# Tuned two-layer decoder kernel: ScalarE reads shared banks first, values between the halves of layer B's keys, both key parts in one product in layer A's first tile

## The chip, the cores and the metric

The kernel runs on one core of one Trainium2 chip. The metric is the device time of one launch in microseconds (us), the median of several runs. A core has five engines with queues of their own: TensorE (PE) multiplies matrices and transposes, and writes into the eight banks of PSUM; ScalarE (ACT) and VectorE (DVE) read those banks and work on tiles in SBUF; GpSimd (POOL) works on SBUF alone; SyncE (SP) issues most of the transfers. Each engine takes its instructions in order and stands still at an instruction whose semaphores are not yet set.

## What is computed

A trunk of two layers on 512 tokens of width 1024. Layer A is latent attention with 8 heads (causal, query blocks of 128), layer B sliding-window attention with 16 query heads on 4 key heads. Each is followed by a layer norm, an MLP with squared ReLU and another layer norm. Cut to what the change touches:

```python
# layer A, one block i of 128 queries of one head
s = einsum('bqhc,bkc->bhqk', ql, c_kv) + einsum('bqhr,bkr->bhqk', qr, k_r)
p = softmax(where(kpos <= qpos, s * scale, -inf))
# layer B
k, v = split(x @ w_kv)          # 4 heads of 64, shared
q = x @ w_q                     # 16 heads of 64
s = einsum(q, k_band) * scale   # block n sees key blocks n-1 and n
p = softmax over (s + bias) and one learned sink per head
```

## The kernel before

Everything is float32 to the eye, but each operand of a product is held as two rounded parts, a high one and a low one (`split`: ScalarE copies the high part, VectorE or GpSimd subtracts it from the source), and a product is made of three: high by high, high by low, low by high (`three`, `group`). PE keeps its program order as it is written (`pe`). On the other engines the builder's scheduler orders the instructions by priority and by what they wait for, and it lets a second engine read a bank only behind the first one's read of it. There are six banks of the tag `mm` and two of the tag `tr` for transposes.

Weights come as a stream of pieces of 128x1024 (`queue`, `weights`): a transfer, a copy to `wh`, a subtraction to `wl`.

Layer A's attention (`scores`, `turn`, `mix` under `run_steps`) goes by head h and query block i. `scores(h, i)` multiplies the queries by n = 128(i+1) keys with five products: `kh` and `kl` with `qh`, `kh` with `ql`, and the rotary parts `khh` and `kll` with `qr`. At i = 0 all five are 128 columns wide. VectorE then adds the mask and takes the maximum in one reduction, and ScalarE takes the exponential.

Layer B begins (`begin`) with two chunks of keys and two of queries, each in two halves of 256 tokens. The first half is multiplied while the last two tiles of tokens are still being turned (`turn_tokens`), in the order keys 0, keys 1, turn 2, queries 0, turn 3, queries 1; then all four second halves, then the values of token tile 0. Values 1 to 3 are fill work in the attention.

Layer B's attention goes by head. I call two heads that share a query chunk a pair, m = 0 to 7 (heads 2m and 2m+1); chunk m of the queries is fill work of two parts of 12 products, 512 columns wide. So PE repeats, for each head, what I call a half: 7 transposes of an earlier head's probabilities (`turn`, L1284 and L1286), 8 products with the values (`mix`), 8 products for the scores of a later head (`scores`), and one part of a query chunk. Behind part 1 stands `query_parts` (L1227, L1228): for each of the two heads ScalarE copies 64 partitions of the bank into `q`, and VectorE subtracts that copy into the other 64. VectorE's work for one head is four reductions with the bias (L1256, one of 128 and three of 256 columns), the bound `nb` (L1260), the low parts `ptl` of the turned probabilities (two pieces, 512 and 384 columns) and the sum `o`. ScalarE's is four exponentials `p` (L1264), the high parts `pth`, and `low`. The last pair, m = 7, has parts of the output projection (`proj`, products of `wh`/`wl` with `oh`/`ol`) as fill in place of queries.

Of the kernel before, what the change touches and what calls it, by code (L numbers as in the profile page):

```python
# [48 lines left out]
def build(tc, nc, io, out):  # L49
    with ExitStack() as top:  # L50
# [231 lines left out]
        first_sq = len(stream)  # L282
        for m in range(8):
            queue("w_sq", io["w_sq"][m], nc.gpsimd if m > 1 else nc.vector, m < 2)
            if m == 1:
                for half_ in range(2):
                    queue("w_v", io["w_v"][half_])
# [70 lines left out]
        for i in range(2):  # L358
            at_hand[i] = raw_tile()
            fetched.add(i)  # L360
            for c in (slice(0, 320), slice(320, 640)) if i == 0 else (slice(0, 640),):
                pe(nc.scalar.dma_start(at_hand[i][:, c], io["w_kv"][i][:, c]))
# [211 lines left out]
        def begin(src, chunks):  # L574


            state["hold"] = len(stream)
            ws = [weights(name) for name, _ in chunks]
            late = []
            for half_ in range(2):  # L580
                cols = slice(half_ * 256, half_ * 256 + 256)
                for i, (_, evac) in enumerate(chunks):
                    b = bank(256)
                    feat_major(src, ws[i], b, cols)
                    late.append((evac, cols, b))
                    if half_ == 0 and i in (1, 2):
                        with tc.high_priority():
                            src.turn(i + 1)
                    if half_ or i > 2:

                        with behind(src.last if not half_ else None):
                            for evac, *at in late:
                                evac(*at)
                        late = []
# [27 lines left out]
        class XFactors(Factors):  # L622
# [14 lines left out]
            def turn(self, t):  # L637

                half_, tk = t // 2, slice(t % 2 * P, (t % 2 + 1) * P)
                if t == NT - 1:  # L640
                    self.b = self.scratch()
                    with tc.issue_after(self.low[1].ins):
                        nc.vector.tensor_sub(self.b, f32(self.xf[0][:, 1]), f32(self.xf[0][:, 0]))
                if t % 2 == 0:
                    self.xf[half_] = self.mp.tile([P, 2, 4, 256], F32R, tag="fac", bufs=3, name=nm("xf"))
                pts = []
                for n in range(2):
                    pt = tbank().rearrange("p (a b) -> p a b", a=4)
                    pts.append(pt)
                    for a in range(4):  # L650
                        k = n * 4 + a
                        pe(nc.tensor.transpose(pt[:, a, :], xs[t][:, k * P : (k + 1) * P], ident))  # L652
                    if half_ == 0:
                        split(self.part(n + 1, 0)[:, :, tk], self.part(n + 1, 1)[:, :, tk], pt)
                    nc.scalar.activation(f32(self.xf[half_][:, n, :, tk]), pt, AF.Copy)
                if half_ == 1:
                    if t % 2 == 0:
                        self.a = self.scratch()
                    nc.vector.tensor_sub(self.a[:, :, tk], pts[0], f32(self.xf[1][:, 1, :, tk]))
                    if t == NT - 1:  # L660
                        nc.vector.tensor_add(self.b[:, :, tk], self.b[:, :, tk], self.a[:, :, tk])
                    self.low = split(self.part(5, 0)[:, :, tk], self.part(5, 1)[:, :, tk], self.a[:, :, tk], keep=True)
                if t == NT - 1:
                    for i in (1, 0):
                        tk = slice(i * P, (i + 1) * P)
                        if i == 0:
                            with tc.issue_after(self.low[1].ins):
                                nc.vector.tensor_add(self.b[:, :, tk], self.b[:, :, tk], self.a[:, :, tk])
                        state["s4"] = split(self.part(3, 0)[:, :, tk], self.part(3, 1)[:, :, tk], self.b[:, :, tk], keep=True)
                    state["hold"] = len(stream)  # L670
# [11 lines left out]
        def mlp(src, gb, dst, mp):  # L682
# [177 lines left out]
            if dst is not None:  # L860
                state["hold"] = first_sq
# [5 lines left out]
        with tc.tile_pool(name="mla", bufs=1) as mp:  # L867
# [9 lines left out]
            khh = mp.tile([P, S], F32R, name="khh")  # L877
            kll = mp.tile([P, S], F32R, name="kll")
# [47 lines left out]
            kr2 = [mp.tile([P, NT, P], F32, tag=("kh", "kl")[a], bufs=2, name=nm("kr2")) for a in range(2)]  # L926

            def rot_key(t, b):
                kr = sp.tile([P, 2, 64], F32, tag="kr", bufs=2, name=nm("kr"))
                rope(kr[:, 0, :], b[:, 256:320], t, 1, kr[:, 1, :])  # L930
                dup = kr[:, 0:1, :].broadcast_to([P, 2, 64])
                hh = kr2[0][:, t, :].rearrange("p (a b) -> p a b", a=2)
                ll = kr2[1][:, t, :].rearrange("p (a b) -> p a b", a=2)
                nc.vector.tensor_copy(hh.bitcast(F32R), dup)
                nc.vector.tensor_sub(ll, dup, hh)
# [41 lines left out]
            for t in range(NT):  # L977
# [12 lines left out]
                if t == 2:  # L990
                    with tc.high_priority():
                        for part, dst in ((0, khh), (1, kll)):
                            pt = tbank()
                            for tt in range(NT):
                                pe(nc.tensor.transpose(pt[:, tt * P : (tt + 1) * P], kr2[part][:, tt, :], ident))
# [22 lines left out]
            def head_keys(h):  # L1018
                heads[h]["w"] = wh, wl = weights("w_h")
                kh = mp.tile([P, S], F32R, tag="kh", bufs=2, name=nm("kh"))  # L1020
                kl = mp.tile([P, S], F32R, tag="kl", bufs=2, name=nm("kl"))
# [4 lines left out]
                split(kh, kl, b)  # L1026
                heads[h]["k"] = kh, kl
# [12 lines left out]
            def pair_rotary(hp):  # L1040

                pt = bank()
                for t in range(NT):
                    pe(nc.tensor.transpose(pt[:, t * P : (t + 1) * P], qrot[t // 2][:, t % 2, hp * P : (hp + 1) * P], ident))  # L1044
                for j, (own, other) in enumerate(((lo, hi), (hi, lo))):
                    qr = mp.tile([P, S], F32R, tag="qr", bufs=3, name=nm("qr"))
                    nc.scalar.activation(qr[own, :], pt[own, :], AF.Copy)
                    nc.vector.tensor_sub(qr[other, :], pt[own, :], f32(qr[own, :]))
                    heads[2 * hp + j]["qr"] = qr
# [25 lines left out]
            def scores(h, i):  # L1075
                a = heads[h]
                kh, kl = a["k"]
# [4 lines left out]
                group(  # L1082
                    b[:, :n],
                    three(qh[:, tq], ql[:, tq], kh[:, :n], kl[:, :n])
                    + [(a["qr"][:, tq], khh[:, :n]), (a["qr"][:, tq], kll[:, :n])],
                )
                if i == 0:
# [5 lines left out]
                    out=b[:, :n], in0=b[:, :n], in1=cmask[:, 512 - n :], op0=ALU.add, op1=ALU.max,  # L1093
# [3 lines left out]
                p = scratch()  # L1097
# [76 lines left out]
        with tc.tile_pool(name="swa", bufs=1) as mp:  # L1174
# [3 lines left out]
            def keys(m, cols, b):  # L1178
                for a, (own, other) in enumerate(((lo, hi), (hi, lo))):
                    j = 2 * m + a  # L1180
                    for to in (own, other):
                        nc.scalar.activation(khh[j][to, cols], b[own, :], AF.Copy)
                        nc.vector.tensor_sub(kll[j][to, cols], b[own, :], f32(khh[j][own, cols]))
# [6 lines left out]
            def values(t):  # L1190
                if t == 0:
                    wv.extend(weights("w_v") for _ in range(2))
                tk = slice(t * P, (t + 1) * P)
                b = bank(256)
                for k in range(KD):
                    wh, wl = wv[k // 4]
                    c = slice(k % 4 * 256, (k % 4 + 1) * 256)
                    group(b, three(x2.h(k, tk), x2.l(k, tk), wh[:, c], wl[:, c]), k == 0, k == 7)
                split(vv[:, t, :, 0:64], vv[:, t, :, 64:P], b.rearrange("p (j d) -> p j d", j=4))
# [13 lines left out]
            def queries(m, part):  # L1213
# [4 lines left out]
                if part == 1:  # L1218
                    load_bias(m)
                    query_parts(m, slice(0, S), b)  # L1220

            def query_parts(m, cols, b):
                if qs[2 * m] is None:
                    qs[2 * m : 2 * m + 2] = [mp.tile([P, S], F32R, tag="q", bufs=4, name=nm("q")) for _ in range(2)]
                for a, (own, other) in enumerate(((lo, hi), (hi, lo))):
                    q = qs[2 * m + a]
                    nc.scalar.activation(q[own, cols], b[own, :], AF.Copy)  # L1227
                    nc.vector.tensor_sub(q[other, cols], b[own, :], f32(q[own, cols]))  # L1228
# [91 lines left out]
            for m in range(2, 8):  # L1320
                for part in range(2):
                    fill.append((2.6, 2 * m - AHEAD_B - 3 + part, -9, lambda m=m, part=part: queries(m, part)))
                if m == 2:
                    for t in range(1, NT):
                        fill.append((2.6, 0, -9, lambda t=t: values(t)))
            for t, kp, u in ((0, 0, 11), (0, 1, 12), (1, 0, 13), (1, 1, 13), (2, 0, 14), (2, 1, 14), (0, 2, 15), (1, 2, 15), (2, 2, 16)):
                fill.append((1.3 if t < 2 else 0, u, u, lambda t=t, kp=kp: proj.part(t, kp)))
            for m in range(2):
                load_bias(m)
            begin(  # L1330
                x2,
                [("w_k", lambda cols, b, m=m: keys(m, cols, b)) for m in range(2)]
                + [("w_sq", lambda cols, b, m=m: query_parts(m, cols, b)) for m in range(2)],
            )
            values(0)
# [118 lines left out]
```

## Time and profile before

| | |
|---|---|
| median of 3 runs | 1004.05 us (1003.70 to 1004.14) |
| the profiled execution | 1003.37 us, its span 1001.6 us |
| TensorE's granted clock | 0.998 |
| PE busy | 989.3 us, 99% of the span |
| DVE, ACT, POOL busy | 771.0, 555.3, 216.0 us |

Busy PE is no measure of PE at its best, since products are pipelined and their ends are modelled. What a product costs is read from the time between two starts. Where that time is longer than between other products of the same widths, PE stood still, and the row says in brackets what ended its wait.

### The profile page before, as it was taken

To read this page: it belongs to the slowest core of one execution; us is meant where nothing else is said; L and a number is where in the kernel's file an instruction comes from. 1 tells how busy PE (TensorE), PEld (TensorE's weight loads), DVE (VectorE), ACT (ScalarE), POOL (GpSimd) and SP (SyncE) were. 2 spreads that over 40 slices of the span, in tenths; PEclk is the share of its full clock that TensorE was granted. 3 is DMA by queue.
4 is the path that set the end of the run, shared out by engine and by line. 5 is a ranking of instruction groups with operands and counts; after the bars stand their busy time and mean duration, and the time that the engine had idled before them with its cause. 6 is when DMAs were issued, how large, how long until landed. Compare 5 with 4: busy or idle time off the path is not lost.

```text
span 1001.6 us, 15947 instructions
## 1 busy us (share of the span) xinstructions
PE 989.3 (99%) x6172; PEld 893.1 (89%) x6172; DVE 771.0 (77%) x1237; ACT 555.3 (55%) x851; POOL 216.0 (22%) x203
## 2 busy tenths in 40 slices
PE   9999999999999999999999999999999999999997
PEld 8888888999999999998899988889998999999986
DVE  5588866989779769886586678698885986898756
ACT  5456643458537637646146788446763764664620
POOL 1231101112212211210003665212122032122000
PEclk9999999999999999999999999999999999999999
DMA  6431126389978977964232212258798798798432
GB/s 247 144 99 43 64 106 210 87 178 243 168 168 227 187 175 203 225 120 135 76 105 96 85 64 75 73 180 199 188 195 185 167 213 171 169 263 146 105 105 84
DMA packets 60392, 149.56 MB, mean 149 GB/s; under 512 B 5228, under 2 KB 10013, under 8 KB 60317
## 3 DMA queue, kind: packets, MB, share of 16 engines
q0 software_dynamic: 24320, 58.73, 32.9%
q1 hardware_dynamic: 35564, 89.16, 26.3%
q8 instruction: 49, 0.80, 0.3%
q10 hardware_dynamic: 432, 0.66, 0.2%
q14 instruction: 27, 0.21, 0.1%
HBM read 146.41 MB, written 4.22 MB: 150 GB/s over the span
## 4 chain that ended last, share of the span: by engine, by line
PE 96%; ACT 2%; DVE 1%; issue 1%; DMA 0%; DVEq 0%; ACTq 0%
PE mm L104 88%; PE tr L104 5%; PE tr L1114 1%; PE tr L652 1%; ACT wh L77 1%; PE tr L1284 0%; ACT p L1264 0%; DMA xraw<-in_xT 0%; PE tr L432 0%; PE tr L1286 0%; ACT q L1227 0%; DVE wl L80 0%; PE mm L1044 0%; PE tr L908 0%; DVE ql L80 0%
## 5 line engine op out<-in xcount | busy, mean ns | idle before, releaser
L104 PE MATMUL mm<-wh,fac 128*128 128x512 f32 (+1 forms) x944 | 292.4, 386 | 0.0
L77 ACT ACTIVATE wh<-wq 128x1024 fp32r<-128x1024 f32 x164 | 173.6, 1060 | 185.5 <-PE mm L104 129.3
L80 DVE TENSOR_TENSOR wl<-wq,wh 128x1024 fp32r<-128x1024 f32 x164 | 199.4, 1220 | 69.4 <-ACT wh L77 68.3
L104 PE MATMUL mm<-xth,wh 128*128 128x256 f32 (+1 forms) x944 | 246.8, 289 | 0.7 <-ACT p L1264 0.7
L104 PE MATMUL mm<-xth,wl 128*128 128x256 f32 (+1 forms) x816 | 236.1, 289 | 0.0
L104 PEld LDWEIGHTS mm<-wh,fac 128*128 128x128 f32 x944 | 176.2, 188 | 35.4 <-DVE fac L80 0.6
L104 PE MATMUL mm<-xtl,wh 128*128 128x256 f32 (+1 forms) x688 | 199.9, 291 | 0.0
L104 PE MATMUL mm<-wl,fac 128*128 128x512 f32 (+1 forms) x472 | 182.3, 386 | 0.0
L104 PEld LDWEIGHTS mm<-xth,wh 128*128 128x128 f32 x944 | 171.7, 192 | 4.1 <-ACT p L1264 1.5
L104 PEld LDWEIGHTS mm<-xth,wl 128*128 128x128 f32 x816 | 156.3, 192 | 2.0
L77 ACT ACTIVATE wh<-raw 128x1024 fp32r<-128x1024 f32 (+4 forms) x85 | 84.7, 998 | 99.0 <-PE mm L104 66.8
L104 PEld LDWEIGHTS mm<-xtl,wh 128*128 128x128 f32 x688 | 131.8, 192 | 2.4
L199 POOL DMA_DIRECT2D wq<-in_up x64 | 77.5, 1228 | 258.8 <-DVE wl L80 192.5
L80 DVE TENSOR_TENSOR wl<-raw,wh 128x1024 fp32r<-128x1024 f32 (+3 forms) x65 | 76.8, 1188 | 38.1 <-ACT wh L77 37.9
L104 PEld LDWEIGHTS mm<-wl,fac 128*128 128x128 f32 x472 | 88.8, 188 | 16.7
L199 POOL DMA_DIRECT2D wq<-in_down x48 | 42.0, 875 | 187.1 <-DVE wl L80 181.2
L80 POOL TENSOR_TENSOR wl<-raw,wh 128x1024 fp32r<-128x1024 f32 (+2 forms) x20 | 41.3, 2071 | 86.7 <-ACT wh L77 84.3
L104 PE MATMUL mm<-wh,oh 128*128 128x512 f32 x128 | 51.1, 399 | 0.9 <-ACT p L1264 0.9
L104 PE MATMUL mm<-wh,ol 128*128 128x512 f32 x128 | 50.1, 392 | 0.0
L104 PE MATMUL mm<-wl,oh 128*128 128x512 f32 x128 | 49.9, 390 | 0.0
L393 POOL TENSOR_TENSOR rs<-mv,half 128x1 f32<-128x1 f32 x16 | 9.9, 620 | 168.2 <-DVE mv L414 168.1
L558 DVE TENSOR_TENSOR x<-mm,x 128x512 f32<-128x512 f32 (+1 forms) x49 | 32.8, 673 | 15.0 <-PE mm L104 15.0
(217 smaller groups left out, 1844.1 us busy)
## 6 DMA issues: line engine op xcount, KB each, us to landing
wq<-in_up POOLq DMA_DIRECT2D x64, 512.0 KB, 8.6
wq<-in_down POOLq DMA_DIRECT2D x48, 512.0 KB, 6.8
wq<-in_up SPq DMA_DIRECT2D x32, 512.0 KB, 7.2
raw<-in_down SPq DMA_DIRECT2D x28, 512.0 KB, 6.6
wq<-in_down SPq DMA_DIRECT2D x24, 512.0 KB, 5.7
raw<-in_up SPq DMA_DIRECT2D x16, 512.0 KB, 4.3
raw<-in_w_o SPq DMA_DIRECT2D x8, 512.0 KB, 3.9
raw<-in_w_sq SPq DMA_DIRECT2D x8, 512.0 KB, 3.3
```

The lines of the kernel that those rows point to most:

```text
L77: high = nc.scalar.activation(dst_h, src, AF.Copy)
L80: low = (engine or nc.vector).tensor_sub(dst_l, src, f32(dst_h))
L104: pe(nc.tensor.matmul(dst, st, mv, start=first and i == 0, stop=last and i == len(pairs) - 1, **kw))
L199: nc.gpsimd.dma_start(half(a, jp), chunk(*more, jp), accum_op=ALU.add)
L393: nc.gpsimd.tensor_tensor(r, v, half, ALU.pow)
L558: nc.vector.tensor_add(xs[t][:, c], b, xs[t][:, c])
L652: pe(nc.tensor.transpose(pt[:, a, :], xs[t][:, k * P : (k + 1) * P], ident))
L1114: pe(nc.tensor.transpose(pt[:, kb * P : (kb + 1) * P], p[:, kb * P : (kb + 1) * P], ident))
```

## The change

Five edits. In layer A the two parts of a head's keys lie in one tile `kk`, and those of the rotary key in one tile `krr`. At i = 0 one product of `qh` with both parts of `kk` writes 256 columns of the bank, one of `qr` with `krr` adds to them, and one of `ql` with the high part adds to the first 128. VectorE adds the second 128 columns and the mask into `p`, and the reduction takes `p` for its mask. At i > 0 the five products stay.

Layer B starts with keys 0 and 1 of the first half; the turns of tiles 2 and 3 have the values of token tiles 0 and 1 between and behind them, half of the inner dimension each; then come the second halves of the keys, then query chunks 0 and 1 whole, 512 columns wide. The weights of the values come ahead of those of the queries in the stream. Values 2 and 3 stay fill work.

Where ScalarE and VectorE both read a bank in several pieces (`XFactors.turn`, `keys`, `query_parts`, `pair_rotary`), ScalarE's pieces all come first, then VectorE's. In layer B's attention `query_parts` has high priority. At the kernel's start the second piece of `w_kv` is fetched on SP's queue, behind the third transfer of `xT`, where it went out on ScalarE's queue before.

```diff
-                kh, kl = a["k"]
+                kk = a["k"]
+                p = scratch()
+                mask = cmask[:, 512 - n :]
+                if i == 0:
+                    two = b[:, 0:256].rearrange("p (a b) -> p a b", a=2)
+                    group(
+                        two, [(qh[:, tq], kk[:, :, :n]), (a["qr"][:, tq], krr[:, :, :n])], True, False,
+                        skip_group_check=True,
+                    )
+                    group(b[:, :n], [(ql[:, tq], kk[:, 0, :n])], False, True, skip_group_check=True)
+                    nc.vector.tensor_add(p[:, :n], b[:, n : 2 * n], mask)
+                    mask = p[:, :n]
...
+            late = products(0)
+            for i, f in enumerate(between):
+                with tc.high_priority():
+                    src.turn(NT - 2 + i)
+                late += f()
+
+            with behind(src.last):
+                for evac, *at in late:
+                    evac(*at)
+            for evac, *at in products(1):
+                evac(*at)
...
                 if part == 1:
                     load_bias(m)
-                    query_parts(m, slice(0, S), b)
+                    with tc.high_priority():
+                        query_parts(m, slice(0, S), b)
...
-                for a, (own, other) in enumerate(((lo, hi), (hi, lo))):
-                    q = qs[2 * m + a]
+                sides = [(qs[2 * m + a], own, other) for a, (own, other) in enumerate(((lo, hi), (hi, lo)))]
+                for q, own, _ in sides:
                     nc.scalar.activation(q[own, cols], b[own, :], AF.Copy)
+                for q, own, other in sides:
                     nc.vector.tensor_sub(q[other, cols], b[own, :], f32(q[own, cols]))
...
-                    for t in range(1, NT):
-                        fill.append((2.6, 0, -9, lambda t=t: values(t)))
+                    for t in range(2, NT):
+                        fill.append((2.6, 0, -9, lambda t=t: more_values(t)))
...
-            begin(
-                x2,
-                [("w_k", lambda cols, b, m=m: keys(m, cols, b)) for m in range(2)]
-                + [("w_sq", lambda cols, b, m=m: query_parts(m, cols, b)) for m in range(2)],
-            )
-            values(0)
+            begin(
+                x2, ["w_k"] * 2, [lambda cols, b, m=m: keys(m, cols, b) for m in range(2)],
+                [lambda half_=half_: first_values(half_) for half_ in range(2)],
+            )
+            for m in range(2):
+                for part in range(2):
+                    queries(m, part)
```

PE, layer A, the first block of a head (`mm` is the bank of the scores), before:

```order
L104 MATMUL mm_743<-cq_170,wl_608 128x512
L104 MATMUL mm_755<-kh_612,qh_695 128x128
L104 MATMUL mm_755<-kl_613,qh_695 128x128
L104 MATMUL mm_755<-kh_612,ql_696 128x128
L104 MATMUL mm_755<-khh,qr_718 128x128
L104 MATMUL mm_755<-kll,qr_718 128x128
L104 MATMUL mm_779<-ckv_h,wh_624 128x512
```

The same place after:

```order
L104 MATMUL mm_739<-cq_169,wl_606 128x512
L104 MATMUL mm_751<-kk_610,qh_692 128x256
L104 MATMUL mm_751<-krr,qr_715 128x256
L104 MATMUL mm_751<-kk_610,ql_693 128x128
L104 MATMUL mm_773<-ckv_h,wh_621 128x512
```

Five products of 128 columns have become two of 256 and one of 128; what stands around them is the same.

DVE, layer B's attention, the half behind the end of query chunk 6 (`q` are its two heads' queries, `ISA` the reductions with the bias, `ptl` the low parts of the turned probabilities), before:

```order
L1260 TENSOR_SCALAR nb_6276<-mm_6279,sink_155 128x4
L1228 TENSOR_TENSOR q_6318<-mm_6235,q_6318 64x512
L80 TENSOR_TENSOR ptl_6325<-tr_6326,pth_6324 128x512
L1256 ISA mm_6356<-mm_6356,bias_6164 128x128
...
L1256 ISA mm_6356<-mm_6356,bias_6164 128x256
...
L1256 ISA mm_6361,mm_6356<-mm_6361,bias_6164 128x256
...
L1256 ISA mm_6361,mm_6356<-mm_6361,bias_6164 128x256
...
L80 TENSOR_TENSOR ptl_6325<-tr_6333,pth_6324 128x384
L1260 TENSOR_SCALAR nb_6353<-mm_6356,sink_155 128x4
L1314 TENSOR_TENSOR o_6263<-mm_6339,low_6348 64x512
L1228 TENSOR_TENSOR q_6319<-mm_6235,q_6319 64x512
```

The same place after:

```order
L1297 ISA mm_6280<-mm_6280,bias_6088 128x128
...
L1297 ISA mm_6280<-mm_6280,bias_6088 128x256
...
L1297 ISA mm_6285,mm_6280<-mm_6285,bias_6088 128x256
...
L1269 TENSOR_TENSOR q_6242<-mm_6159,q_6242 64x512
L1269 TENSOR_TENSOR q_6243<-mm_6159,q_6243 64x512
L1297 ISA mm_6285,mm_6280<-mm_6285,bias_6088 128x256
...
L80 TENSOR_TENSOR ptl_6249<-tr_6250,pth_6248 128x512
L80 TENSOR_TENSOR ptl_6249<-tr_6257,pth_6248 128x384
L1355 TENSOR_TENSOR o_6187<-mm_6263,low_6272 64x512
L1301 TENSOR_SCALAR nb_6277<-mm_6280,sink_155 128x4
```

The first subtraction for the queries stood ahead of the reductions and the second behind `o`; now both stand behind the third reduction, and ahead of both pieces of `ptl`.

DVE, the same half of the last pair, behind query chunk 7 (`wl` is a piece of the projection's weights), before:

```order
L80 TENSOR_TENSOR wl_6535<-raw_6533,wh_6534 128x1024
L1228 TENSOR_TENSOR q_6470<-mm_6387,q_6470 64x512
L80 TENSOR_TENSOR ptl_6477<-tr_6478,pth_6476 128x512
L1256 ISA mm_6508<-mm_6508,bias_6316 128x128
...
L1256 ISA mm_6508<-mm_6508,bias_6316 128x256
...
L1256 ISA mm_6513,mm_6508<-mm_6513,bias_6316 128x256
...
L80 TENSOR_TENSOR ptl_6477<-tr_6485,pth_6476 128x384
L1314 TENSOR_TENSOR o_6415<-mm_6491,low_6500 64x512
```

The same place after:

```order
L1297 ISA mm_6432<-mm_6432,bias_6240 128x128
...
L80 TENSOR_TENSOR wl_6459<-raw_6457,wh_6458 128x1024
L1297 ISA mm_6432<-mm_6432,bias_6240 128x256
...
L1269 TENSOR_TENSOR q_6394<-mm_6311,q_6394 64x512
L1269 TENSOR_TENSOR q_6395<-mm_6311,q_6395 64x512
L80 TENSOR_TENSOR ptl_6401<-tr_6402,pth_6400 128x512
L1297 ISA mm_6437,mm_6432<-mm_6437,bias_6240 128x256
...
L80 TENSOR_TENSOR ptl_6401<-tr_6409,pth_6400 128x384
```

`wl` and the first subtraction stood ahead of the reductions; now `wl` stands behind the first reduction, and both subtractions behind the second.

## Rows read from the trace of the kernel before

**Rows 1.** The page: busy time of the engines, and the chain that ended last.
```profile
PE 989.3 (99%) x6172; PEld 893.1 (89%) x6172; DVE 771.0 (77%) x1237; ACT 555.3 (55%) x851; POOL 216.0 (22%) x203
...
PE 96%; ACT 2%; DVE 1%; issue 1%; DMA 0%; DVEq 0%; ACTq 0%
```

**Rows 2.** PE's waits, whole span: total us, times, longest us.
```profile
PE mm L104 <- ACT p L1264: 1.6, 6, 0.7
```

**Rows 3.** Timeline of PE, layer A's first block: start, duration, instruction, [idle before, releaser].
```profile
80.31 0.30 PE L104 MATMUL mm<-kh,qh 128*128 128x128 f32 x1
80.45 0.28 PE L104 MATMUL mm<-kl,qh 128*128 128x128 f32 x1
80.56 0.28 PE L104 MATMUL mm<-kh,ql 128*128 128x128 f32 x1
80.67 0.27 PE L104 MATMUL mm<-khh,qr 128*128 128x128 f32 x1
80.78 0.27 PE L104 MATMUL mm<-kll,qr 128*128 128x128 f32 x1
```

**Rows 4.** Timeline of PE, second halves at the start of layer B.
```profile
524.28 0.28 PE L104 MATMUL mm<-xth,wh 128*128 128x256 f32 x1
524.40 0.28 PE L104 MATMUL mm<-xtl,wh 128*128 128x256 f32 x1
```

**Rows 5.** Timeline of PE, one half of layer B's attention, from its first transpose.
```profile
605.28 0.27 PE L1284 MATMUL tr<-ident,p 128*128 128x128 f32 x1
...
607.92 0.40 PE L104 MATMUL mm<-xth,wh 128*128 128x512 f32 x1
608.15 0.40 PE L104 MATMUL mm<-xtl,wh 128*128 128x512 f32 x1
...
610.67 0.27 PE L1284 MATMUL tr<-ident,p 128*128 128x128 f32 x1
```

**Rows 6.** Timeline of PE, layer B's attention, three places where it stands still.
```profile
601.97 0.28 PE L104 MATMUL mm<-skl,q 128*128 128x256 f32 x1
602.43 0.50 PE L104 MATMUL mm<-xth,wh 128*128 128x512 f32 x1 [0.18 <-ACT p L1264]
...
615.46 0.27 PE L1286 MATMUL tr<-ident,p 128*128 128x128 f32 x1
616.33 0.30 PE L1284 MATMUL tr<-ident,p 128*128 128x128 f32 x1 [0.60 <-DVE ptl L80]
...
622.52 0.28 PE L104 MATMUL mm<-skl,q 128*128 128x256 f32 x1
623.50 0.50 PE L104 MATMUL mm<-wh,oh 128*128 128x512 f32 x1 [0.71 <-ACT p L1264]
```

**Rows 7.** Timeline of DVE, the same stretch.
```profile
601.13 0.69 DVE L1228 TENSOR_TENSOR q<-mm,q 64x512 fp32r<-64x512 f32 x1 [1.32 <-ACT q L1227]
601.85 0.69 DVE L80 TENSOR_TENSOR ptl<-tr,pth 128x512 fp32r<-128x512 f32 x1
602.46 0.29 DVE L1256 CUSTOM_DVE_ANT_0 mm<-mm,bias 128x128 f32<-128x128 f32 x1
...
602.79 0.43 DVE L1256 CUSTOM_DVE_ANT_0 mm<-mm,bias 128x256 f32<-128x256 f32 x1
...
603.37 0.43 DVE L1256 CUSTOM_DVE_ANT_0 mm<-mm,bias 128x256 f32<-128x256 f32 x1
...
607.64 0.30 DVE L1256 CUSTOM_DVE_ANT_0 mm<-mm,bias 128x128 f32<-128x128 f32 x1
...
608.94 0.42 DVE L1256 CUSTOM_DVE_ANT_0 mm<-mm,bias 128x256 f32<-128x256 f32 x1
...
609.28 0.56 DVE L80 TENSOR_TENSOR ptl<-tr,pth 128x384 fp32r<-128x384 f32 x1
...
611.73 1.22 DVE L80 TENSOR_TENSOR wl<-raw,wh 128x1024 fp32r<-128x1024 f32 x1 [0.70 <-ACT wh L77]
```

**Rows 8.** Timeline of ACT, the same stretch.
```profile
600.51 0.59 ACT L1227 ACTIVATE q<-mm 64x512 fp32r<-64x512 f32 x1
```

**Rows 9.** Timeline of PE, the kernel's start.
```profile
10.87 0.31 PE L104 MATMUL mm<-wh,xth 128*128 128x320 f32 x1
11.20 0.41 PE L104 MATMUL mm<-wl,xth 128*128 128x320 f32 x1
```

More of the change, by code (lines that the diff above doesn't have):

```diff
@@ L281, in build @@
             queue("w_k", io["w_k"][m])
-        first_sq = len(stream)
+        first_v = len(stream)
+        for half_ in range(2):
+            queue("w_v", io["w_v"][half_], after=True)
         for m in range(8):
[L284 to L287, printed above, removed]
+            queue("w_sq", io["w_sq"][m], nc.gpsimd if m > 1 else nc.vector)
         for c in range(8):
@@ L356, in build @@
         state["hold"] = len(stream)
[L358 to L362, printed above, removed]
+        at_hand[0] = raw_tile()
+        fetched.add(0)
+        for c in (slice(0, 320), slice(320, 640)):
+            pe(nc.scalar.dma_start(at_hand[0][:, c], io["w_kv"][0][:, c]))
         prep(0, 2, lambda j: load_x(j, 1))
@@ L572, in feat_major, with begin, products @@
                 group(dst, three(wh[:, kc], wl[:, kc], src.h(k, cols), src.l(k, cols)), k == 0, k == KD - 1)
-        def begin(src, chunks):
+        def begin(src, names, evacs, between):
             state["hold"] = len(stream)
[L578 to L582, printed above, removed]
+            ws = [weights(name) for name in names]
+            def products(half_):
+                late = []
+                for w, evac in zip(ws, evacs):
+                    cols = slice(half_ * 256, half_ * 256 + 256)
                     b = bank(256)
-                    feat_major(src, ws[i], b, cols)
+                    feat_major(src, w, b, cols)
                     late.append((evac, cols, b))
[L586 to L594, printed above, removed]
+                return late
+            late = products(0)
[8 more added lines that the diff above has]
+                evac(*at)
         class Factors:
@@ L860, in mlp @@
             if dst is not None:
[L861 removed]
+                state["hold"] = first_v
             TokMajor(Hidden(), add_last, "down").finish(gb, dst, dst and (0, 0, 0, 1))
@@ L923, in rope @@
                 nc.vector.tensor_add(dst, dst, other)
-            kr2 = [mp.tile([P, NT, P], F32, tag=("kh", "kl")[a], bufs=2, name=nm("kr2")) for a in range(2)]
+            kr2 = mp.tile([P, 2, NT, P], F32, tag="kk", bufs=2, name=nm("kr2"))
             def rot_key(t, b):
@@ L994, in build @@
                             for tt in range(NT):
-                                pe(nc.tensor.transpose(pt[:, tt * P : (tt + 1) * P], kr2[part][:, tt, :], ident))
+                                pe(nc.tensor.transpose(pt[:, tt * P : (tt + 1) * P], kr2[:, part, tt, :], ident))
                             nc.scalar.activation(dst, pt, AF.Copy)
@@ L1019, in head_keys @@
                 heads[h]["w"] = wh, wl = weights("w_h")
-                kh = mp.tile([P, S], F32R, tag="kh", bufs=2, name=nm("kh"))
-                kl = mp.tile([P, S], F32R, tag="kl", bufs=2, name=nm("kl"))
+                heads[h]["k"] = kk = mp.tile([P, 2, S], F32R, tag="kk", bufs=2, name=nm("kk"))
                 b = bank()
@@ L1044, in pair_rotary @@
                     pe(nc.tensor.transpose(pt[:, t * P : (t + 1) * P], qrot[t // 2][:, t % 2, hp * P : (hp + 1) * P], ident))
+                qr = [mp.tile([P, S], F32R, tag="qr", bufs=3, name=nm("qr")) for _ in range(2)]
+                for j, own in enumerate((lo, hi)):
+                    nc.scalar.activation(qr[j][own, :], pt[own, :], AF.Copy)
                 for j, (own, other) in enumerate(((lo, hi), (hi, lo))):
[L1046 to L1049, printed above, removed]
+                    nc.vector.tensor_sub(qr[j][other, :], pt[own, :], f32(qr[j][own, :]))
+                    heads[2 * hp + j]["qr"] = qr[j]
             values_in()
```

68 lines of the change are left out of this document (40 added, 28 removed).

## The prediction

> **What bounds the kernel now.** I read the page's chain first: PE carries 96% of it and is busy 99% of the span [rows 1]. So a part of the change counts if it takes time from PE's own row of products, or moves one of the few places where PE stands still. Then I read PE's waits: the largest entry is ScalarE's exponential of layer B's attention, 1.6 us in six waits [rows 2]. Last comes the timeline around these waits, for the work that is queued ahead of what PE wants.
>
> A wait is measured start to start. Between two products of 256 columns 0.12 us pass [rows 4], and a 512-column product also starts about 0.12 behind one of 256. At 601.97 it took 0.46 [rows 6]: 0.34 of waiting, and some 0.1 more because the product after a pause is longer, 0.50 for 0.40 [rows 5, 6]. So 0.45, and five of the six waits look alike, one for each of the pairs 3 to 7. The sixth is 0.98 at 622.52, about 0.95 above the normal step; ahead of it stand 0.87 at 615.46, where transposes wait for `ptl`, 0.76 above their 0.11 [rows 6]. Layer B's attention thus loses 5 x 0.45 + 0.76 + 0.95, about 4.0 us. There is as much to lose there as to gain.
>
> **Layer A's first block.** Five products of 128 columns follow each other at 0.11 [rows 3]; two of 256 and one of 128 take 2 x 0.12 + 0.11 = 0.35 for 0.55. That is 0.20 for each of 8 heads: -1.6 us, on PE itself. No row shows a right-hand operand in two pieces; at i = 0 each piece is one run of 128 columns, so I take 0.12, with nothing gained as the other end (0.22, two products of 128). VectorE gets 8 additions of 128 columns, about 0.3 each by the 128-column reduction [rows 7]. What waits for them is the exponential, whose block is turned only three blocks later, so I cost them at nothing; uncovered they would be 8 x 0.3 = 2.4.
>
> The Trainium skill gives two paces ("TensorE: Matmul & The Clock Gate", Back-to-back issue gap): an isolated product takes N/2.4 + 2.5 ns, and a sustained stream about 81 ns for 128 columns and 131 for 512. By the first, joining products would gain almost nothing here; by the second the queries below alone would gain some 3 us. This trace agrees with neither: 110 ns for 128 columns, 120 for 256, 229 for 512. The rows decide.
>
> **Layer B's start.** The two query chunks were 96 products of 256 columns, 11.5 us at 0.12. Now they are 48 of 512: 12 took 2.75 us, from 607.92 to 610.67 [rows 5], so 48 take 11.0: -0.5. The values of tile 1 only move ahead. The values do between the turns what the first query halves did, and their weights have the old place in the stream. The second key half needs what it needed; the first query chunk then needs weights whose buffer comes free when keys 0 end, 2.9 us (24 x 0.12) ahead; a copy and a subtraction (1.22, [rows 7]) fit in with some 0.4 to spare. If that cover is gone it costs the shortfall, hardly over 0.5. Scores 0 want queries 0, which end one whole chunk (5.5 us) earlier. I cost this at nothing.
>
> **Layer B's attention.** In the half behind a query chunk's end I count from its first transpose. The scores' first reduction starts at 2.36 (605.28 to 607.64), and the next half is due at 5.39 (605.28 to 610.67) [rows 5, 7]. Before, the first subtraction for the queries ran ahead of the reductions, where VectorE had been idle 1.32 us, and the second much later [rows 7]; ScalarE's second copy waited for the first subtraction, so the query bank stayed taken and the next chunk waited for a scores bank, that is for the exponential. After, both copies stand together, and in the order of pairs 5 and 6 both subtractions stand behind the third reduction and ahead of `ptl`. The next half's transposes wait for `ptl`, since they write the bank that it reads. By the steps of rows 7: 2.36, then 0.33 and 0.58 to the third reduction, 0.34 to the subtractions, 2 x 0.72, 0.34 for the fourth reduction, 0.61 for `ptl`: 6.0. PE waits 0.6 where it waited 0.45: +0.17 for each of pairs 5 and 6. In pair 3 the exponential keeps its place, with one copy more ahead of it (up to 0.59, [rows 8]): +0.5. In pair 4 the copies fall behind the exponential, and by the same count 0.2 remains: -0.25.
>
> Pair 7 is the worst. `wl` (1.22) stood in the idle time ahead of the reductions [rows 7]; now it stands behind the first, with both subtractions behind the second: 2.36 + 0.33 + 1.2 + 0.34 + 1.44 + 0.61 = 6.3, while PE, with only six products of projection between (6 x 0.23), is there at about 4.0. That is 2.3, then 0.35 for the second piece of `ptl`, and about 0.7 of the later wait for the exponential: 3.35 against 0.45 + 0.76 + 0.95 = 2.15, so +1.2. The attention together: 0.5 - 0.25 + 0.35 + 1.2 = **+1.8**. Its bounds: -2.25 if the five waits go and nothing takes their place, +3 if the subtractions also delay the exponentials.
>
> **The start.** The second piece of `w_kv` no longer competes with the third transfer of `xT`, so that copy can start sooner. Of this PE sees the step at 10.87, 0.33 where 0.15 is normal [rows 9]: -0.2. If the piece itself comes late by one issue, it is +0.4.
>
> **Reader order elsewhere.** PE has no wait over 0.1 at the two turns to the MLPs or at the keys; the subtractions that come one copy (about 0.6) later have over 1 us until their products. Nothing.
>
> **Sum.** -1.6 - 0.5 + 1.8 - 0.2 = -0.5. The profiled execution took 1003.37, so 1002.9; the median stands 0.7 above it: **1003.5**.
>
> **Rivals.** (a) *The attention loses nothing*: the scheduler's new order leaves no wait longer than the old. Then the total is -2.3 and better: 1001.7 at an attention of 0, 999.5 with the five waits gone. For it: the query bank is really freed sooner. Against it: VectorE's order in pairs 5 to 7. It is faster by the bound if the attention costs under +0.3. Chance 0.27.
>
> (b) *VectorE becomes the bound of the pairs*: in each of the five pairs the two subtractions (1.44) come wholly on PE's path, since `nb`, the exponential and GpSimd's scaling also wait behind them. That is 5 x 1.44 for 5 x 0.45, +5.0, and +1.2 at the end: in all 6.2 - 2.3, so 1008. It is slower than before once the pairs and the end lose 2.3, slower by the bound from 4.3. Against it: VectorE has time to spare in each pair, 1.32 us ahead of one subtraction alone [rows 7]. Chance 0.07.
>
> (c) *Joining does not pay*: a product costs by its columns, or one in two pieces costs two. Then -1.6 is lost: 1005.1. The page's first pace is of this kind. Against it: 0.11 and 0.12 in rows 3 and 4. Chance 0.05.
>
> **How the numbers follow.** My forecast, within 1002.1 to 1005, has 0.61. Under 0.2% (2.0 us) nothing can be told from no change. Faster by more: 0.27, from (a); slower by more: 0.07, from (b); the same: 0.61 + 0.05. The range for 8 in 10 reaches into (a) and ends below (b): 1000.9 to 1005.3.
>
> **What would show it.** In the profile after: two 256-column steps of 0.12 and one of 0.11 in layer A's first block; 24 products of 512 columns in a row for each of query chunks 0 and 1 without a pause at either front; in the attention waits of transposes for `ptl` in pairs 5 and 6 (about 0.6 each) and one over 2 us in pair 7, where the exponential's waits were. If those transposes do not wait, my reading of VectorE's queue is wrong, and (a) holds. If PE waits for the exponential in every pair, (b) does.

## The result, and the profile after

The kernel after takes **1006.73 us** (1005.99 to 1007.43, 10 runs) where the kernel before took 1003.98 beside it (10 runs): ratio **1.0026**, interval 1.0016 to 1.0036. It is slower by 2.75 us. The forecast of 1003.5 was wrong, and the time lies above the range.

The page of the kernel after, and PE's waits (total us, times, longest us):

```profile
PE 986.9 (98%) x6108; PEld 889.4 (89%) x6108; DVE 774.8 (77%) x1241; ACT 555.4 (55%) x847; POOL 217.1 (22%) x203
...
PE 93%; DVE 3%; ACT 1%; DMA 1%; issue 1%; POOL 0%; DVEq 0%; POOLq 0%; ACTq 0%
```

```profile
PE tr L1325 <- DVE ptl L80: 5.4, 5, 3.3
...
PE mm L104 <- ACT p L1305: 0.9, 1, 0.9
```

PE does 64 products fewer and is busy 2.4 us less than in [rows 1], yet the span grew from 1001.6 to 1004.4 us. In the chain PE's share fell from 96 to 93%, and VectorE's rose from 1 to 3%. The six waits for the exponential of [rows 2] have become one, and in their place stand five waits of the transposes for `ptl`, 5.4 us together (before, one of 0.6). So I looked first at what came before these waits, then at the waits.

**What was gained.** Layer A's first block after the change, on PE, for the head of [rows 3]:

```profile
79.96 0.36 PE L104 MATMUL mm<-kk,qh 128*128 128x256 f32 x1
80.16 0.28 PE L104 MATMUL mm<-krr,qr 128*128 128x256 f32 x1
80.28 0.22 PE L104 MATMUL mm<-kk,ql 128*128 128x128 f32 x1
```

From `krr` to the next start 0.12 pass, as between products of 256 columns in one piece. The block's three products take 0.38 (79.96 to 80.34), where the five took 0.58 (80.31 to 80.89): 0.20 for each head, as forecast. The product `mm<-wh,oh` that starts at 176.37 before starts at 174.53 after: 1.84 us earlier. Layer B's first two query chunks are now 48 products of 512 columns in a row, at 0.23 to 0.24 each (528.64 to 539.55), without a pause at either front:

```profile
528.64 0.40 PE L104 MATMUL mm<-xth,wh 128*128 128x512 f32 x1
528.88 0.40 PE L104 MATMUL mm<-xtl,wh 128*128 128x512 f32 x1
```

The last scores product ahead of the first wait starts at 565.96 (below) where it started at 568.33 before:

```profile
568.33 0.28 PE L104 MATMUL mm<-skl,q 128*128 128x256 f32 x1
```

By then the change is 2.37 us ahead, of which 0.5 came since 499 us. These two terms are as forecast.

**What was lost.** PE in layer B's attention, the same places as in [rows 6], one fence for pairs 3 to 7 (the idle time and its releaser in brackets):

```profile
565.96 0.28 PE L104 MATMUL mm<-skl,q 128*128 128x256 f32 x1
567.17 0.50 PE L104 MATMUL mm<-xth,wh 128*128 128x512 f32 x1 [0.93 <-ACT p L1305]
...
581.18 0.30 PE L1325 MATMUL tr<-ident,p 128*128 128x128 f32 x1 [0.23 <-DVE ptl L80]
...
592.99 0.30 PE L1325 MATMUL tr<-ident,p 128*128 128x128 f32 x1 [0.82 <-DVE ptl L80]
...
604.78 0.30 PE L1325 MATMUL tr<-ident,p 128*128 128x128 f32 x1 [0.82 <-DVE ptl L80]
...
614.02 0.39 PE L104 MATMUL mm<-wh,ol 128*128 128x512 f32 x1
617.75 0.30 PE L1325 MATMUL tr<-ident,p 128*128 128x128 f32 x1 [3.34 <-DVE ptl L80]
...
618.11 0.27 PE L1327 MATMUL tr<-ident,p 128*128 128x128 f32 x1
618.56 0.30 PE L1325 MATMUL tr<-ident,p 128*128 128x128 f32 x1 [0.18 <-DVE ptl L80]
```

Start to start, over the normal step, these are 1.1 (1.2 with the longer product behind it), 0.39, 0.97, 0.97, and in pair 7 3.50 and 0.35. That is 7.3 us. The last wait of [rows 6] is gone.

Then TensorE's clock falls. Busy time of the engines by stretch, with PEclk as the granted clock:

```profile
614.00:617.50 3.50, 0.41 (x2) 0.00 (x0) 3.42 (x6) 1.18 (x3) 0.03 (x1) 1.00 0.38 109
617.50:619.00 1.50, 1.07 (x8) 0.89 (x9) 1.47 (x5) 0.53 (x1) 0.00 (x0) 1.00 0.25 101
619.00:621.00 2.00, 2.00 (x12) 2.00 (x11) 1.76 (x6) 1.66 (x6) 1.13 (x1) 0.51 0.00 0
621.00:622.30 1.30, 1.30 (x8) 1.30 (x8) 0.31 (x2) 1.30 (x7) 0.15 (x1) 0.50 0.06 13
622.30:626.00 3.70, 3.70 (x27) 3.39 (x27) 3.24 (x12) 2.30 (x8) 1.82 (x2) 0.98 0.00 0
```

In the first stretch PE does two products and stands. From 619.0 to about 622.4 the granted clock is 0.50, the 1.2 GHz level (the last stretch has 0.98, so its first tenth of a microsecond or two are still low), and products of 256 columns follow each other at 0.21 instead of 0.12. From the first value product behind the transposes to the first of `mm<-wh,oh` it takes 3.39 us. The same stretch took 1.94 in a run at full clock (`e4` below, second profile). Both, after first:

```profile
618.83 0.39 PE L104 MATMUL mm<-pth,vv 128*128 128x256 f32 x1
...
622.22 0.50 PE L104 MATMUL mm<-wh,oh 128*128 128x512 f32 x1
```

```profile
617.97 0.36 PE L104 MATMUL mm<-pth,vv 128*128 128x256 f32 x1
...
619.91 0.39 PE L104 MATMUL mm<-wh,oh 128*128 128x512 f32 x1
```

So the clock costs 1.45 there.

Together 7.3 + 0.1 + 1.45, about 8.8, where before lost 4.0: **+4.8** against the forecast of +1.8. With -2.37 this is +2.5, close to the span's +2.8. Read from start to start over the whole attention the loss is 5.1 more than before: its last value product starts at 641.13 where it started at 638.38, 2.75 later, though PE had been 2.37 ahead. From there to the end the two traces keep this distance, so all of the loss lies in the attention.

Why pair 7 waits so long is seen on VectorE and GpSimd, the stretch of [rows 7]:

```profile
612.58 0.30 DVE L1297 CUSTOM_DVE_ANT_0 mm<-mm,bias 128x128 f32<-128x128 f32 x1 [0.55 <-PE mm L104]
...
612.80 2.31 DVE L80 TENSOR_TENSOR wl<-raw,wh 128x1024 fp32r<-128x1024 f32 x1
615.03 0.42 DVE L1297 CUSTOM_DVE_ANT_0 mm<-mm,bias 128x256 f32<-128x256 f32 x1
...
615.49 1.39 DVE L1269 TENSOR_TENSOR q<-mm,q 64x512 fp32r<-64x512 f32 x2
616.91 0.69 DVE L80 TENSOR_TENSOR ptl<-tr,pth 128x512 fp32r<-128x512 f32 x1
```

```profile
612.56 1.47 POOL L1314 TENSOR_TENSOR p<-p,ri 128x768 f32<-128x768 f32 x1
```

The order is the one counted out in the prediction: reduction, `wl`, reduction, both query subtractions, `ptl`. But `wl` takes 2.31 instead of 1.22. GpSimd's scaling of the probabilities began 0.24 us ahead of it and ends at 614.03; `wl` ends 1.08 behind that. By these times `wl` did most of its work only when GpSimd was done. The 220 subtractions of 128x1024 for `wl` in this trace that meet no GpSimd arithmetic have a median of 1.22, and none is over 1.23. The Trainium skill says the same ("SBUF — State Buffer", SBUF: two separate sides): a VectorE operation with two inputs in SBUF and a GpSimd operation that reads SBUF share one pair of ports, which whoever begins first holds for its whole instruction. This trace agrees: 2.31 for 1.22. The kernel before shows it too, in a place that I didn't read (VectorE, then GpSimd):

```profile
643.46 1.99 DVE L80 TENSOR_TENSOR wl<-raw,wh 128x1024 fp32r<-128x1024 f32 x1 [0.25 <-ACT wh L77]
```

```profile
642.56 1.81 POOL L80 TENSOR_TENSOR ol<-o,oh 128x512 fp32r<-128x512 f32 x1 [6.48 <-ACT oh L77]
```

It goes both ways there: GpSimd's `ol` itself began inside an earlier `wl` of VectorE (641.99 to 643.22) and took 1.81, where the other `ol` of the attention take 1.29 or 1.30.

**Pairs 5 and 6.** VectorE again, from the third reduction to `ptl`:

```profile
601.71 0.43 DVE L1297 CUSTOM_DVE_ANT_0 mm<-mm,bias 128x256 f32<-128x256 f32 x1
...
602.18 1.39 DVE L1269 TENSOR_TENSOR q<-mm,q 64x512 fp32r<-64x512 f32 x2
603.60 0.43 DVE L1297 CUSTOM_DVE_ANT_0 mm<-mm,bias 128x256 f32<-128x256 f32 x1
...
603.95 1.15 DVE L80 TENSOR_TENSOR ptl<-tr,pth 128x512 fp32r<-128x512 f32 x2
```

From the third reduction to the subtractions 0.47 pass, where I took 0.34, and PE's transposes start 0.83 behind the start of `ptl` (603.95 to 604.78), where I took 0.61 for its first half. These two small steps are the 0.35 by which the wait was underrated.

**The start.** The step at 10.87 of [rows 9] is gone:

```profile
10.81 0.31 PE L104 MATMUL mm<-wh,xth 128*128 128x320 f32 x1
10.96 0.31 PE L104 MATMUL mm<-wl,xth 128*128 128x320 f32 x1
```

At 28 us PE is 0.34 ahead. But in this execution the transposes at 47 us wait longer for `cq` on VectorE (0.23 idle before, 0.47 after), and at layer A's first block, 64 us, nothing of it is left. Tenths of a microsecond at this place go with the execution: two kernels without the new fetch (`t1` and `q1` below) are 0.46 and 0.44 ahead of before at 38 us, though both still have the step near 10.8.

### The profile page after: what moved, and what is told of

It is laid out like the page before. It is cut to its first block, busy times and chain, and to the rows that moved or that the text cites. A ratio compares the mean times of both kernels' runs of the same rounds, so it can differ in the third digit from the quotient of the medians.

```text
span 1004.4 us, 15823 instructions
## 1 busy us (share of the span) xinstructions
PE 986.9 (98%) x6108; PEld 889.4 (89%) x6108; DVE 774.8 (77%) x1241; ACT 555.4 (55%) x847; POOL 217.1 (22%) x203
## 4 chain that ended last, share of the span: by engine, by line
PE 93%; DVE 3%; ACT 1%; DMA 1%; issue 1%; POOL 0%; DVEq 0%; POOLq 0%; ACTq 0%
PE mm L104 85%; PE tr L104 5%; PE tr L1135 1%; PE tr L656 1%; DVE mm L1297 1%; PE tr L1325 1%; ACT wh L77 0%; PE tr L1327 0%; DVE q L1269 0%; DVE wl L80 0%; DMA xraw<-in_xT 0%; DMA raw<-in_w_qr 0%; PE tr L430 0%; DVE ptl L80 0%; DMA raw<-in_w_h 0%
## 5 line engine op out<-in xcount | busy, mean ns | idle before, releaser
L104 PE MATMUL mm<-xth,wh 128*128 128x256 f32 (+1 forms) x928 | 243.5, 290 | 0.9 <-ACT p L1305 0.9
L104 PE MATMUL mm<-xth,wl 128*128 128x256 f32 (+1 forms) x800 | 233.2, 292 | 0.0
L104 PE MATMUL mm<-xtl,wh 128*128 128x256 f32 (+1 forms) x672 | 197.1, 293 | 0.0
L104 PEld LDWEIGHTS mm<-xth,wh 128*128 128x128 f32 x928 | 168.6, 192 | 4.3 <-ACT p L1305 1.1
L104 PEld LDWEIGHTS mm<-xth,wl 128*128 128x128 f32 x800 | 153.2, 192 | 2.6
L104 PEld LDWEIGHTS mm<-xtl,wh 128*128 128x128 f32 x672 | 128.7, 191 | 3.0
```

The source lines that it names most:

```text
L104: pe(nc.tensor.matmul(dst, st, mv, start=first and i == 0, stop=last and i == len(pairs) - 1, **kw))
```

## The experiments

The theory (A): the order of the query chunks' readers, ScalarE's copies first and both subtractions behind them, costs the 5 us in layer B's attention, and the other edits are worth what was forecast. The rivals: (B) other edits also cost; (C) in pair 7 the cause is `wl` and not the queries; (D) it isn't VectorE's queue at all, but the copies that delay ScalarE's exponentials. Times are medians, and each ratio is to the kernel before on the same chip (1003.8 to 1004.2).

**1. The queries' readers as before, all else as after.** The edit of `e1`:

```diff
-                    with tc.high_priority():
-                        query_parts(m, slice(0, S), b)
+                    query_parts(m, slice(0, S), b)
...
-                for q, own, _ in sides:
-                    nc.scalar.activation(q[own, cols], b[own, :], AF.Copy)
                 for q, own, other in sides:
+                    nc.scalar.activation(q[own, cols], b[own, :], AF.Copy)
                     nc.vector.tensor_sub(q[other, cols], b[own, :], f32(q[own, cols]))
```

> The changed kernel with one edit undone: in query_parts each head's copy is followed by its own subtraction again, and without high priority; all other edits stay. Theory A (the loss is the order of the query subtractions on VectorE, about 5.0 us of layer B's attention): 1001.6, that is 2.4 below the kernel before; no wait of the transposes for ptl over 1 us, the five waits of 0.45 for the exponential back. Rival B (the loss comes from the new start of layer B, which leaves the attention one values block less as fill): 1005 to 1007, with the long wait in pair 7 still there.

Measured: **1001.74** (9 runs), ratio 0.9974, 0.9964 to 0.9984. PE's waits in this run:

```profile
PE mm L104 <- ACT p L1303: 1.6, 6, 0.7
...
PE tr L430 <- DVE xtl L80: 0.8, 1, 0.8
PE tr L1323 <- DVE ptl L80: 0.6, 1, 0.6
```

The six waits of [rows 2] are back, the long one for `ptl` is gone, and the kernel is 2.3 us faster than before and 5.0 faster than after. (A) holds in size, and (B) falls. The edit takes back the order and the high priority together; the next run has the new order without the priority.

**2. That order alone, in the kernel before.** The edit of `q1`:

```diff
-                for a, (own, other) in enumerate(((lo, hi), (hi, lo))):
-                    q = qs[2 * m + a]
+                sides = [(qs[2 * m + a], own, other) for a, (own, other) in enumerate(((lo, hi), (hi, lo)))]
+                for q, own, _ in sides:
                     nc.scalar.activation(q[own, cols], b[own, :], AF.Copy)
+                for q, own, other in sides:
                     nc.vector.tensor_sub(q[other, cols], b[own, :], f32(q[own, cols]))
```

> The kernel before with one part of the change alone: in query_parts ScalarE's two copies first, then VectorE's two subtractions. Theory A: the loss of layer B's attention alone, +5.0, so 1009.0, with the long wait for ptl in pair 7 and a fallen clock behind it. Rival B (the order costs only together with the new start of layer B): 1004 to 1005.

Measured: **1009.87** (5 runs), ratio 1.0053, 1.0040 to 1.0065: +5.9 us. The long waits of after are all there (four for `ptl`, 5.2 us together, and the one for the exponential, 0.9), and the clock falls at the longest here too (the wait, then busy time and PEclk by stretch):

```profile
621.04 0.45 PE L1285 MATMUL tr<-ident,p 128*128 128x128 f32 x1 [3.35 <-DVE ptl L80]
```

```profile
619.00:621.00 2.00, 0.00 (x0) 0.00 (x0) 1.96 (x4) 0.00 (x0) 0.00 (x0) 0.69 0.76 250
621.00:623.00 2.00, 1.96 (x10) 1.90 (x11) 1.88 (x7) 0.78 (x2) 0.00 (x0) 0.50 0.03 12
623.00:626.00 3.00, 3.00 (x16) 3.00 (x16) 1.77 (x6) 2.33 (x8) 1.28 (x1) 0.50 0.00 0
626.00:627.00 1.00, 1.00 (x5) 0.82 (x5) 0.86 (x4) 1.00 (x5) 0.00 (x0) 0.72 0.00 0
```

and `wl` took 2.32 beside GpSimd's scaling here as well. One edit of the change, without the priority, costs what the whole change lost, and more. Part of the more is the clock: by these shares it is at 0.50 for 6.8 us (619.75 to 626.55), twice as long as in after.

**3. `wl` taken out of pair 7's queue.** In `e4` the fourth piece of `w_so` is subtracted by GpSimd, all else as after:

```diff
-POOL_O, POOL_SO = (0, 2), (0, 1, 2)
+POOL_O, POOL_SO = (0, 2), (0, 1, 2, 3)
```

> The changed kernel with one piece of the projection's weights (the fourth of w_so) subtracted on GpSimd, not on VectorE, so that it no longer stands ahead of the query subtractions in pair 7. Theory A: the wait of 3.5 us in pair 7 falls to about 1.3, and the granted clock, which in the changed kernel fell to 0.5 for some 3 us behind that wait, stays at 1.0: -2.3 - 1.5, so 1002.9. Rival C (the clock falls for another reason than the long wait, as the busy share of the stretch before): the wait is shorter but the clock still falls: 1004.4.

Measured: **1004.58** (11 runs, 1002.91 to 1006.65), ratio 1.0005, 0.9997 to 1.0014: 2.1 us of after's loss is back. In the profiled execution (1003.25) the transposes in pair 7 wait 2.34 over the normal step, not 3.85, and the clock stays up behind it:

```profile
616.33 0.30 PE L1325 MATMUL tr<-ident,p 128*128 128x128 f32 x1 [2.18 <-DVE ptl L80]
```

```profile
619.00:622.00 3.00, 3.00 (x23) 2.69 (x22) 2.56 (x13) 2.95 (x12) 1.81 (x3) 1.00 0.03 8
```

So `wl` is part of pair 7's wait, and a wait of 2.2 us was not followed by a lower clock, where one of 3.3 was, and one of 3.4 lay in the fall. (C) holds as a part: 1.5 us of waiting and 1.45 of clock in this execution, but 2.3 remain without `wl` (the fourth reduction now stands ahead of `ptl` too). The executions lie in two groups, six up to 1004.6 with a mean granted clock of 0.998 over the execution, and five from 1005.5 on with 0.996 to 0.997. To see the upper one I profiled the kernel a second time:

> The same kernel as the one with the fourth piece of w_so on GpSimd, profiled a second time. Its executions lay in two groups, 1002.9 to 1004.6 and 1005.5 to 1006.7, and the profiled one (1003.25, a wait of 2.3 us in pair 7 and an undisturbed clock) was of the lower. If the upper group is executions in which TensorE's clock falls after that wait, a profiled execution above 1005 shows a granted clock near 0.5 between 616 and 622 us, and one below 1004.6 shows 1.0 there. If a profiled execution above 1005 shows 1.0 there, the two groups have another cause.

Measured: 1004.35, with the same wait (2.18 idle) and 1.00 from 614 to 624 us. It is of the lower group again. That the clock falls in the upper one is what their mean clock suggests; no trace shows it, and it stays open.

**4. The subtractions behind `ptl`.** If the queue ahead of `ptl` is all, the subtractions of chunks 2 to 7 can go behind the next half's `ptl` and the new order should even gain. In `e6` (the calls of chunks 2 to 7 pass `later`, and the priority is gone):

```diff
...
-                for q, own, other in sides:
-                    nc.vector.tensor_sub(q[other, cols], b[own, :], f32(q[own, cols]))
+                def subs():
+                    for q, own, other in sides:
+                        nc.vector.tensor_sub(q[other, cols], b[own, :], f32(q[own, cols]))
+
+                if later:
+                    late_subs.append(subs)
...
+                while late_subs:
+                    with behind(low_part):
+                        late_subs.pop(0)()
```

> The changed kernel with all its edits, but the two query subtractions of chunks 2 to 7 put behind both pieces of ptl of the next turned head on VectorE. Theory A (the loss is what stands ahead of ptl in VectorE's queue, not that ScalarE reads first): the waits of 0.97 in pairs 5 and 6 go, pair 7 keeps about 1.3 (wl and four reductions ahead of ptl), the clock stays at 1.0, the attention loses 1 to 3 us in all: 1000.5 to 1002.5. Rival D (ScalarE reading first is itself the loss, since its second copy delays the exponentials by 0.5 in each pair and PE then waits for a scores bank): waits for the exponential of about 0.95 in each of five pairs, 1004 or more.

Measured: **1004.75** (11 runs), ratio 1.0005, 0.9996 to 1.0014. My expectation missed. The waits for `ptl` are gone but for one, but others stand in their place:

```profile
PE mm L104 <- ACT p L1312: 2.8, 4, 0.9
...
PE mm L104 <- DVE o L1365: 1.1, 1, 1.1
PE tr L1332 <- DVE ptl L80: 0.7, 1, 0.7
```

PE waits for the exponential in four of the pairs 3 to 7, by 1.09 over the normal step in pairs 4 and 6 and 0.6 in pairs 5 and 7, where it waited 0.34 in each before. ScalarE ahead of the wait in pair 4:

```profile
575.75 1.20 ACT L1268 ACTIVATE q<-mm 64x512 fp32r<-64x512 f32 x2
...
577.47 0.36 ACT L1312 ACTIVATE p<-mm,nb 128x128 f32<-128x128 f32 x1
```

The exponential starts 1.72 behind the first copy's start. In pair 3 of before it was 0.97 (566.87 to 567.84), with one copy between. That is 0.75 later, and PE's wait is 0.75 longer. So (D) holds in part too: two copies in a row ahead of ScalarE's exponential delay the bank that PE wants next, as in pair 3 of after (1.72 again, 564.49 to 566.21). Of the orders tried here the old one, with a subtraction between the copies, is the best.

**5. The other edits, one by one, in the kernel before.** The joined products alone (`t1`, the diff of layer A's first block):

> The kernel before with layer A's first-block edit alone (both key parts in one product, one addition more on VectorE). By the prediction's term -1.6, so 1002.4; by the two traces, where the last layer A product runs 1.5 earlier after than the edit's start would give, -1.5 to -1.9. Rival (the additions on VectorE give some of it back in the softmax): above 1003.

Measured: **1002.87** (11 runs), ratio 0.9988, 0.9979 to 0.9996: -1.14 us; in the trace the product at 176.37 starts at 174.38, and of these 1.99 us PE was 0.37 ahead already at layer A's first block (64 us), so -1.6 for the edit. The start of layer B alone (`s1`: `begin`, the values between the halves of the keys, the keys' readers):

> The kernel before with the change's start of layer B alone: two query chunks as 48 products of 512 columns instead of 96 of 256, the values of the last two tiles between the halves of the keys, and the readers of the keys with ScalarE first. The queries keep their old order. By the term of the prediction -0.5 us, so about 1003.5 where the kernel before has 1004.0, and no wait of PE longer than before at the start of layer B (524 to 545 us). If the first query chunk has to wait for its weights it would be 0 or slower.

Measured: 1004.92 (11 runs, 1003.42 to 1005.97), ratio 1.0006, 0.9997 to 1.0015: no difference that can be told, and not the -0.5. Its profiled execution (1005.65) has a wait at this start:

```profile
PE tr L431 <- DVE xtl L80: 0.5, 1, 0.5
```

PE is 0.19 us ahead of before up to 517 us, stands 0.6 for `xtl`, and at 568 is 0.11 behind: without that wait it gained 0.3. The wait for `xtl` is there in the profiled executions of `e1` (0.96), `e6` (0.62) and `t1` (0.43), which has the old start, and in the second of `e4` (0.45), but not in the others, after among them, so it goes with the execution. Two waits for `fac` at 953 and 955 us, 1.7 over the normal step, are far from the edit. What the start of layer B is worth alone thus lies, by the interval, between 0.3 us gained and 1.5 lost. The fetch at the start alone (`f1`):

> The kernel before with the start's fetch alone: the second piece of w_kv on SP's queue behind the third transfer of xT. The prediction has -0.2: 1003.8. By the two traces PE is 0.34 earlier at 28 us and gives it back in longer waits for cq at 47 us and at 60 us: 1004.0. Rival: the piece comes late and costs 0.4: 1004.4.

Measured: 1003.76 (11 runs), ratio 0.9998, 0.9988 to 1.0007: no difference that can be told. In its trace the step near 10.8 is gone, PE is 0.41 ahead at 38 us and level with before at 230. By their ratios the three alone add up to -0.8 us, where `e1`, which has all three, has -2.6; each interval reaches about 0.9 to either side, so beyond the joined products it stays open what each gives to `e1`. And `e1` with the turns to the MLPs and layer A's rotated queries read in the old order as well (`e8`):

> The kernel with the query pieces as before, and with the order of readers as before also in the turns to the MLPs and in the rotary queries; joined products, layer B's start, the keys' order and the fetch stay as changed. The prediction costs these two at nothing: 1001.7, the same within 0.1%. Rival: they gave something, then 1002.5 or more; or they cost something, 1001.0 or less.

Measured: 1001.40 (9 runs), ratio 0.9972, 0.9963 to 0.9982, the same as `e1` within the noise. In these two places, where PE doesn't wait behind it, the order of readers makes no difference that can be told.

**6. The good parts and `wl` on GpSimd.** `e7` is `e1` with the one-line edit of `e4`:

> The kernel with the query pieces as before (all other edits of the change), and with the fourth piece of w_so subtracted on GpSimd. Theory A: wl and a query subtraction stand ahead of ptl in pair 7 and cost the 0.77 there; without wl it goes: 1001.0, 0.7 below the same kernel with wl on VectorE. Rival E (GpSimd's 2.4 us for the piece delay the scaling of the probabilities, and PE waits for that): 1001.7 or more.

Measured: **1000.50** (5 runs), ratio 0.9965, 0.9952 to 0.9978. It beats both kernels: 3.7 us faster than before, 6.2 faster than after. Against `e1` it is 1.2 by the medians, and the two intervals overlap. PE's waits for the exponential are 0.9 in five (they were 1.6 in six), since the last and longest, 0.7 idle at 622.52 in [rows 6], is gone. The expectation had named another: the transposes' wait in pair 7, 0.60 idle with `ptl` before, has become 0.44 (the profile puts it down to `nb`), so most of it stayed.

```profile
PE mm L104 <- ACT p L1303: 0.9, 5, 0.2
```

## Why the prediction was wrong

**Right.** The place to look (PE's few waits in layer B's attention, with as much to lose as to gain); the joined products, -1.6 forecast, -1.84 in the trace and -1.14 as a median alone, so that rival (c) falls; the mechanism of the loss: VectorE reaches `ptl` later, PE's transposes wait, pair 7 is the worst. The order counted out for pairs 5 to 7 is the order in the trace. Rival (a) falls with it. Rival (b) gave the right sign and nearly the size, 1008, but by another way: the pairs lose less than it said (5 and 6: 0.97 each, not 1.44) and pair 7 far more.

**The layer B start** is -0.5 in after's trace, and alone no difference that can be told. **The fetch** takes its step at 11 us away and is worth no difference that can be told: I stopped at the first wait that it takes away, and the sum of -0.2 is smaller than what this place varies by between executions.

**Wrong: the attention's term, +1.8 for +4.8.** By its own steps:

| step | forecast | trace of after |
|---|---|---|
| pair 3, wait | 0.95 | 1.2 |
| pair 4 | 0.2 | 0.39 |
| pairs 5 and 6, each | 0.6 | 0.97 |
| pair 7, for `ptl` | 2.3 + 0.35 | 3.50 + 0.35 |
| pair 7, later wait | 0.7 | none |
| clock behind pair 7 | none | 1.45 |
| all, against 4.0 before | 5.8 | 8.8 |

Three things were missed. First, in the count for pair 7 `wl` was priced at its own 1.22 (the 1.2 of that sum), though in its new place it falls beside GpSimd's scaling: 2.31, so 1.1 more. The kernel before shows such a meeting at 643.46, and I took only `wl`'s mean. Second, I priced a wait of 2 to 3 us at its length; behind one of 3.5 the clock was at half for 3.4 us. The later wait, forecast at 0.7, did not come, which pays for half of that. Third, pairs 3 to 6 were short by 0.2 to 0.4 each, in pair 3 because the second copy delayed the exponential by 0.75 and not by 0.5, in pairs 5 and 6 by two steps from one engine to another that I took at 0.1 and 0.2 too little; together 1.2 us. The upper bound of the attention, +3, was a sum of waits again and had no room for the first two; with +4.8 in its place the working gives 1006.6, close to the measured 1006.73.

## What to carry to other kernels

When an edit moves an instruction on one engine, look at what runs on the neighbour engine at its new place, not only at its duration at the old one: a subtraction cost 2.31 us instead of 1.22 beside GpSimd. Two readers of one bank that alternate between engines free neither engine's queue in one piece, and that can be the better order when both queues also carry what TensorE waits for. Bound a new wait of several microseconds on TensorE from above by more than its length, since products behind it may run at the lower clock: here they did behind waits of 3.3 us, and not behind 2.2.

## What the runs showed that I had not expected

- A subtraction on VectorE with both inputs in SBUF (128x1024) that starts inside a GpSimd operation ends about 1.1 us behind that one's end: 2.31 in after, 2.32 in `q1`, 1.99 in before, for 1.22 alone. The other way round, a GpSimd subtraction that starts inside a VectorE one took 1.81 for 1.29. The prediction's `wl` was one of two in after's trace that met it so.
- With a wait of 3.3 to 3.5 us on TensorE its granted clock fell to 0.50, in after 1.3 us behind the wait's end (619.0 to 622.4), in `q1` already within the wait, and to 626.5. With one of 2.2 it stayed at 1.00 (`e4`, both profiles).
- A right-hand operand of two pieces of 128 columns costs TensorE what one of 256 does: 0.12 from `krr` to the next start.
